# Index scores of a sparse-attention layer: the sum over heads moved from VectorE into PSUM, by products with diagonal matrices

## The chip, the cores and the metric

The kernel runs on one core of a Trainium2 chip. A core has five engines, each with its own in-order queue: TensorE (PE, matrix products; its weight loads are listed apart as PEld), VectorE (DVE), ScalarE (ACT), GpSimd (POOL) and SyncE (SP, which here only issues DMAs). The metric is the device time of one execution in microseconds, lower is better. TensorE is granted one of two clocks, 1.2 or 2.4 GHz; the profile gives the mean granted clock of a stretch as a share of the full one.

## The reference, cut to what matters

A decoder trunk of two layers works on 1024 tokens of width 1024, with 16 meta tokens ahead of them (1040 rows), in float32. The first layer picks, for every query, its 256 best keys by an index score, and then attends to those keys only. The changed part is the score:

```python
logits = jnp.einsum('qhd,sd->qhs', qi_blk, ki_s)              # 8 index heads of 64
score = jnp.einsum('qh,qhs->qs', w_blk, jax.nn.relu(logits))  # signed weight per query and head
score = jnp.where(causal, score, -jnp.inf)
_, idx = lax.top_k(score, topk)
```

A query block has 128 queries. Block b (0 to 7) sees L[b] = 16 + 128(b+1) keys. Block 0 needs no selection, so scores are computed for blocks 1 to 7, over 272, 400, 528, 656, 784, 912 and 1040 keys (4592 together).

## The kernel before

The program is written as Python generators (one per piece of work) that a helper, `weave`, pulls in turn in proportion to their number of steps. A scheduler then fixes the order in each engine's queue; tile pools with a given number of buffers decide what must wait for what.

The score stage, L538 to L549, weaves three things:

- `index(c)`: for the key and query columns of chunk c (three chunks of some 346 rows), five projections (L188, groups of 24 products: one "ki" and four "qi"). Each is copied out of PSUM (`raw_...`), rotated (`rope`, L344: four DMAs that swap halves into a `rot` tile, two POOL multiplications L350 and L351, an addition L352), and split into a high and a low float32r part, `kih`/`kil` and `qis` (ACT copies at L130, DVE subtractions L403 and L404).
- `scores(b)`, L441: for each head and each piece of at most 400 keys, two products L447 and L448 into a bank of tag "pt" (three buffers), a ReLU on ACT (L450) that multiplies by the absolute weight `wab`, into a tile `tm` (three buffers), and one DVE instruction that multiplies by the sign `wsg` and adds to the scores in SBUF (L452 for head 0, L454 for the others). At the end of a block DVE adds the causal mask to the last 128 columns (L458).
- with the last three blocks, the two projections of the attention keys (`k_evac`), whose norm needs a float32 product with the constant `sel` (L263) into a "pt" bank, then two ACT and four DVE instructions (L268 to L281; the bank is free after L276), and the first four rounds of `threshold(1, 5)`.

`threshold` finds the 256th best score of each row bit by bit: 31 rounds of counts (L470 on DVE for most blocks, L487 on ACT for blocks 3, 4 and 6), each round using the result of the last (L492, L493, L489). After the score stage, L550 weaves the other rounds of blocks 1 to 4, 16 rounds of blocks 5 to 7 and the eight query projections. Masks and attention follow.

PSUM has eight banks, four of tag "ps" (projections), three "pt", one "po". A plain float32 product appears in the trace as two records of L263 or L1300 each; a float32r product as one.

Of the kernel before, what the change touches and what calls it, by code (L numbers as in the profile page):

```python
# [10 lines left out]
F32 = mybir.dt.float32  # L11
# [3 lines left out]
OP = mybir.AluOpType  # L15
PSUM = bass.MemoryType.PSUM

P = 128
# [10 lines left out]
IH = 8  # L29
# [20 lines left out]
L = [NMETA + P * (b + 1) for b in range(NB)]  # L50
# [23 lines left out]
def chunks_of(n):  # L74
    parts = -(-n // 400)
    size = -(-n // parts)
    size += size % 2
    out, s = [], 0
    while s < n:
        out.append((s, min(size, n - s)))  # L80
        s += size
    return out
# [3 lines left out]
def trunk(ctx: ExitStack, tc: tile.TileContext, x, meta_tokens, attn_norm, mlp_norm, mlp_w1, mlp_w2,  # L86
          a_w_in, a_q_gain, a_k_gain, a_w_out, kv_norm, kv_w, kv_f_bias, kv_k_gain,
          b_w_q, b_q_gain, b_w_out, rope_cos, rope_sin, out):
    nc = tc.nc
    x = x[0]  # L90
    out = out[0]
# [13 lines left out]
    def bank(tag="ps"):  # L105
        n_ps[0] += 1
        return psum["p"].tile([P, 512], F32, tag=tag, name=f"ps{n_ps[0]}", bufs={"ps": 4, "pt": 3, "po": 1}[tag])
# [21 lines left out]
    def copy(dst, src, scale=1.0):  # L129
        nc.scalar.activation(dst, src, AF.Copy, scale=scale)  # L130
# [120 lines left out]
    HWID = SQW  # L251
# [42 lines left out]
    def scs(b):  # L294
        return sc[:, SC_OFF[b]:SC_OFF[b] + L[b]]
# [6 lines left out]
                            base=0, channel_multiplier=1)  # L302
# [37 lines left out]
    with tc.tile_pool(name="inw", bufs=2, reuse_waits="tile") as iw:  # L340
# [3 lines left out]
        def rope(src, dst, rows, name, s, m):  # L344
            rot = iw.tile([P, HWID], F32, tag="rot", name=f"rot{name}_{s}", bufs=3)[0:rows, 0:m]
            src, c, sn = src[0:rows, 0:m], rc[0:rows, s:s + m], rs[0:rows, s:s + m]
            for q in range(0, rows, 32):
# [6 lines left out]
        trifar = iw.tile([P, P], F32, name="trifar", bufs=1)  # L354
        nc.vector.memset(trifar, 0.0)
        nc.gpsimd.affine_select(out=trifar, in_=trifar, pattern=[[-1, P]], compare_op=OP.is_ge, fill=FAR,
                                base=0, channel_multiplier=1)
# [3 lines left out]
        wsg = iw.tile([P, NB, IH], F32, name="wsg", bufs=1)  # L361
        wab = iw.tile([P, NB, IH], F32, name="wab", bufs=1)

        def raw_tile(name, s):
            return iw.tile([P, HWID], F32, tag="raw", name=f"raw_{name}_{s}", bufs=5)

        def ends(s):
            return s == CH_A[-1][0]
# [1 line left out]
        def ki_evac(o, s, m):  # L370
            raw = raw_tile("ki", s)
            cs = slice(s, s + m)
            copy(raw[0:HD, 0:m], o[0:HD, 0:m])
            copy(wi[:, cs], o[HD:HD + IH, 0:m])
            rope(raw, raw[0:HD, 0:m], HD, "ki", s, m)
            split(kih[0:HD, cs], kil[0:HD, cs], raw[0:HD, 0:m])
            nc.sync.dma_start(f32(kih[HD:P, cs]), f32(kih[0:HD, cs]))
            nc.sync.dma_start(f32(kil[HD:P, cs]), f32(kil[0:HD, cs]))
            bs = [b for b in range(1, NB) if s < L[b] <= s + m]
            b0, b1 = bs[0], bs[-1] + 1  # L380

            def post():
                wt = bank("pt")
                for b in bs:
                    t0 = NMETA + P * b
                    nc.tensor.transpose(wt[:, b * IH:b * IH + IH], wi[:, t0:t0 + P], ident[0:IH, 0:IH])
                wv = wt[:, b0 * IH:b1 * IH].rearrange("p (b h) -> p b h", h=IH)
                sg, ab = wsg[:, b0:b1], wab[:, b0:b1]
                nc.vector.tensor_scalar(sg, wv, 0.0, 2.0, OP.is_ge, OP.mult)
                nc.vector.tensor_scalar(sg, sg, -1.0, None, OP.add)  # L390
                nc.vector.scalar_tensor_tensor(ab, wv, IH ** -0.5 * HD ** -0.5, sg, OP.mult, OP.mult)
            return post

        def qi_evac(mi):
            def evac(o, s, m):
                raw = raw_tile(f"qi{mi}", s)
                copy(raw[:, 0:m], o[:, 0:m])
                rope(raw, raw[:, 0:m], P, f"qi{mi}", s, m)
                e, o = s3[:, 2 * mi, s:s + m], s3[:, 2 * mi + 1, s:s + m]
                r0, r1 = raw[0:HD, 0:m], raw[HD:P, 0:m]  # L400
                copy(e[0:HD], r0)
                copy(o[HD:P], r1)
                nc.vector.tensor_tensor(e[HD:P], r0, f32(e[0:HD]), OP.subtract)  # L403
                nc.vector.tensor_tensor(o[0:HD], r1, f32(o[HD:P]), OP.subtract)  # L404
            return evac

        def k_evac(mi):
            def evac(o, s, m):
                raw = raw_tile(f"k{mi}", s)
                rest = head_norm(iw, o, s, m, G_AK, raw[:, 0:m], sqa[:, s:], 1)  # L410

                def post():
                    rest()
                    rope(raw, ka[:, mi, s:s + m], P, f"k{mi}", s, m)
                return post
            return evac
# [22 lines left out]
            return evac  # L439

        def scores(b):  # L441
            sb = scs(b)
            t0 = NMETA + P * b
            for h in range(IH):
                for s, m in chunks_of(L[b]):
                    o = bank("pt")
                    nc.tensor.matmul(o[:, 0:m], s3[:, h, t0:t0 + P], kih[:, s:s + m], start=True, stop=False)  # L447
                    nc.tensor.matmul(o[:, 0:m], s3[:, h, t0:t0 + P], kil[:, s:s + m], start=False, stop=True)  # L448
                    tm = iw.tile([P, 400], F32, tag="tm", name=f"tm{b}_{h}_{s}", bufs=3)
                    nc.scalar.activation(tm[:, 0:m], o[:, 0:m], AF.Relu, scale=wab[:, b, h:h + 1])  # L450
                    if h == 0:
                        nc.vector.tensor_scalar(sb[:, s:s + m], tm[:, 0:m], wsg[:, b, h:h + 1], None, OP.mult)  # L452
                    else:
                        nc.vector.scalar_tensor_tensor(sb[:, s:s + m], tm[:, 0:m], wsg[:, b, h:h + 1],  # L454
                                                       sb[:, s:s + m], OP.mult, OP.add)
                if h % 2:
                    yield
            nc.vector.tensor_tensor(sb[:, L[b] - P:], sb[:, L[b] - P:], trifar, OP.add)  # L458

        cand = att_in.tile([P, 2, NB], I32, name="cand")  # L460
        flip = att_in.tile([P, NB], I32, name="flip", bufs=1)
# [75 lines left out]
        nc.sync.dma_start(rs, rope_sin)  # L537
        weave((islice(pre, 3), 3), (index(0), 5))  # L538
        weave((pre, 2), (index(1), 5), (scores(1), 4))
        weave((index(2), 5), (chain(*[scores(b) for b in range(2, 5)]), 12))  # L540
        for i, g in enumerate((a_q_gain[0], a_k_gain[0], kv_k_gain, b_q_gain[0])):
            for half in range(2):
                nc.sync.dma_start(gains[HD * half:HD * half + HD, i:i + 1], g.rearrange("(p o) -> p o", o=1))
        rqb.append(bank("po"))
        va = att_in.tile([P, NW, AG, P], F32R, tag="va", name="va")
        thr1, thr2 = threshold(1, 5), threshold(5, NB)
        weave((chain(*[scores(b) for b in range(5, NB)]), 12),
              (chain(*[a_gemm(QW + mi * P, P, k_evac(mi), fine=True) for mi in range(2)]), 18),
              (islice(thr1, T1), T1))  # L549
# [547 lines left out]
    with tc.tile_pool(name="bw", bufs=2, reuse_waits="tile") as bw:  # L1097
# [95 lines left out]
        def qkv(t):  # L1193
            return chain(q_gemm(t), k_gemm(t), v_gemm(t))
# [123 lines left out]
        for u, (h, half, pr) in enumerate(units):  # L1318
# [5 lines left out]
            if half == 0 and h % 2 == 0:  # L1324
                if u:
                    run(fill)
                fill = qkv(t + 1) if t + 1 < NK else iter(())
# [67 lines left out]
```

## Time and profile before

| what | value |
|---|---|
| median of three timed runs | 2973.07 us (2971.38 to 2973.3) |
| profiled execution, its own time | 2966.22 us |
| its span, first to last instruction | 2964.4 us |
| busy in the span: PE / DVE / ACT / POOL | 2721.3 / 2109.0 / 1483.8 / 1309.8 us |
| mean granted TensorE clock | 0.96 |

The profiled execution is a single one; 1.8 us of its time lie outside its span, and it is 6.85 us under the median. Shares of busy time are means over very different stages: the score stage is the first 7% of the span. The recorded duration of a product includes its way through the array, so that the next one begins before it ends; how much of TensorE a product takes is seen in the distance from its start to the next start.

### The profile page before, as it was taken

To read this page: it belongs to the slowest core of one execution; us is meant where nothing else is said; L and a number is where in the kernel's file an instruction comes from. 1 tells how busy PE (TensorE), PEld (TensorE's weight loads), DVE (VectorE), ACT (ScalarE), POOL (GpSimd) and SP (SyncE) were. 2 spreads that over 40 slices of the span, in tenths; PEclk is the share of its full clock that TensorE was granted. 3 is DMA by queue.
4 is the path that set the end of the run, shared out by engine and by line. 5 is a ranking of instruction groups with operands and counts; after the bars stand their busy time and mean duration, and the time that the engine had idled before them with its cause. 6 is when DMAs were issued, how large, how long until landed. Compare 5 with 4: busy or idle time off the path is not lost.

```text
span 2964.4 us, 46393 instructions
## 1 busy us (share of the span) xinstructions
PE 2721.3 (92%) x16666; PEld 2390.6 (81%) x16666; DVE 2109.0 (71%) x4186; ACT 1483.8 (50%) x2828; POOL 1309.8 (44%) x1199
## 2 busy tenths in 40 slices
PE   6889788999889999999988999999897999989999
PEld 6779656778879998999978888888775788867777
DVE  7899989984664547666776778878857555567774
ACT  5767577885333334333434666666643333333332
POOL 2346344531455565222434555555515565542321
PEclk9999779999979999999999999999998999999999
DMA  5312200003224445444511111111322344454442
GB/s 171 78 46 70 52 19 1 1 1 101 79 90 155 147 141 194 137 123 129 157 61 49 51 51 51 51 51 51 101 64 68 124 157 146 149 181 151 148 135 71
DMA packets 243158, 281.96 MB, mean 95 GB/s; under 512 B 22272, under 2 KB 183872, under 8 KB 242928
## 3 DMA queue, kind: packets, MB, share of 16 engines
q1 hardware_dynamic: 242928, 279.01, 30.5%
q8 instruction: 131, 2.15, 0.3%
q14 instruction: 99, 0.81, 0.1%
HBM read 192.42 MB, written 67.63 MB: 88 GB/s over the span
## 4 chain that ended last, share of the span: by engine, by line
PE 55%; DVE 19%; DMA 8%; ACT 6%; issue 5%; POOL 5%; SPq 0%; POOLq 0%; ACTq 0%; DVEq 0%
PE ac L958 32%; PE ps L175 6%; DMA ld<-rdr 5%; PE ps L188 5%; DVE sc L470 3%; PE ps L697 2%; PE ps L662 2%; PE ps L1281 2%; PE ps L1303 2%; PE ps L717 1%; PE ps L720 1%; ACT bp L1259 1%; PE ps L1248 1%; DVE g L137 1%; DVE opc L137 1%
## 5 line engine op out<-in xcount | busy, mean ns | idle before, releaser
L958 PE MATMUL ac<-opc,g 128*128 128x260 f32 (+1 forms) x3456 | 580.6, 324 | 35.7 <-ACT q L130 12.0
L958 PEld LDWEIGHTS ac<-opc,g 128*128 128x128 f32 x3456 | 505.4, 192 | 94.9 <-ACT q L130 14.2
L958 PE MATMUL ac<-opb,g 128*128 128x260 f32 (+1 forms) x2304 | 390.1, 325 | 48.5 <-ACT opb L130 31.1
L958 PEld LDWEIGHTS ac<-opb,g 128*128 128x128 f32 x2304 | 336.3, 191 | 93.4 <-ACT opb L130 36.7
L958 PE MATMUL ac<-opa,g 128*128 128x260 f32 (+1 forms) x2304 | 396.1, 325 | 6.4 <-DVE osqa L238 4.4
L958 PEld LDWEIGHTS ac<-opa,g 128*128 128x128 f32 x2304 | 342.1, 193 | 42.5 <-DVE osqa L238 4.8
L950 POOL TENSOR_TENSOR t<-rb,t 128x512 f32<-128x512 f32 x128 | 190.9, 1491 | 342.8 <-DMA rb<-in_mlp_w_dram 270.6
L137 DVE TENSOR_TENSOR g<-t,g 128x512 fp32r<-128x512 f32 x256 | 224.3, 876 | 134.1 <-ACT g L130 131.4
L130 ACT ACTIVATE g<-t 128x512 fp32r<-128x512 f32 x256 | 161.0, 629 | 262.4 <-PE ac L958 156.9
L188 PE MATMUL ps<-xhb,wh 128*128 128x256 f32 (+5 forms) x640 | 208.6, 326 | 3.3 <-DVE z L1110 2.1
L188 PE MATMUL ps<-xhb,wl 128*128 128x256 f32 (+5 forms) x640 | 197.7, 309 | 0.0
L188 PE MATMUL ps<-xlb,wh 128*128 128x256 f32 (+5 forms) x640 | 196.8, 308 | 0.0
L950 POOL TENSOR_TENSOR t<-ra 128x512 f32<-128x512 f32 x64 | 98.3, 1535 | 179.5 <-DVE g L137 174.2
L137 DVE TENSOR_TENSOR g<-rb,g 128x512 fp32r<-128x512 f32 x128 | 111.7, 872 | 57.1 <-ACT g L130 57.0
L662 PE MATMUL ps<-ks,qs 128*128 128x264 f32 (+7 forms) x544 | 127.3, 347 | 24.7 <-DVE qs L588 12.7
L1239 POOL TENSOR_SCALAR bp<-bcb,cq 128x528 f32<-128x528 f32 (+7 forms) x128 | 103.6, 812 | 98.7 <-PE ps L1281 49.5
L130 ACT ACTIVATE bth<-ps 128x512 fp32r<-128x512 f32 (+4 forms) x224 | 110.5, 496 | 66.5 <-PE ps L1281 62.1
L1303 PE MATMUL ps<-bth,bvs 128*128 128x512 f32 (+2 forms) x420 | 134.3, 397 | 6.2 <-DVE qb L1310 5.0
L130 ACT ACTIVATE q<-ac 128x520 f32<-128x520 f32 (+1 forms) x96 | 57.6, 600 | 163.8 <-PE ac L958 158.8
L188 PEld LDWEIGHTS ps<-xhb,wh 128*128 128x128 f32 x640 | 122.5, 191 | 18.6 <-issue 9.8
L1263 POOL TENSOR_SCALAR bp<-bp,bnm 128x400 f32<-128x400 f32 (+7 forms) x128 | 101.1, 801 | 80.0 <-DVE bnm L1261 80.0
L130 ACT ACTIVATE wh<-wr 128x1024 fp32r<-128x1024 f32 (+1 forms) x84 | 87.4, 1040 | 93.8 <-PE ps L175 61.0
(353 smaller groups left out, 6775.4 us busy)
## 6 DMA issues: line engine op xcount, KB each, us to landing
ra<-in_mlp_w_dram SPq DMA_DIRECT2D x64, 512.0 KB, 3.9
rb<-in_mlp_w_dram SPq DMA_DIRECT2D x64, 512.0 KB, 4.3
ld<-rdr SPq DMA_DIRECT2D x56, 520.0 KB, 4.2
ld<-rdr SPq DMA_DIRECT2D x56, 512.0 KB, 4.0
rdr<-q SPq DMA_DIRECT2D x64, 260.0 KB, 2.0
rdr<-q SPq DMA_DIRECT2D x64, 256.0 KB, 2.3
rdr<-qs SPq DMA_DIRECT2D x48, 260.0 KB, 2.0
wr<-in_a_w_in_dram SPq DMA_DIRECT2D x24, 512.0 KB, 4.1
```

What stands on the lines that cost most here:

```text
L130: nc.scalar.activation(dst, src, AF.Copy, scale=scale)
L137: (nc.gpsimd if pool else nc.vector).tensor_tensor(lo, src, f32(hi), OP.subtract)
L175: nc.tensor.matmul(o[0:n, 0:m], a[:, k, 0:n], b[:, k, s:s + m], start=(k == 0 and j == 0), stop=(k == NK - 1 and j == 2))
L188: nc.tensor.matmul(o[0:n, 0:m], a[:, k, 0:n], b[:, k, s:s + m], start=(k == 0 and j == 0), stop=(k == NK - 1 and j == 2))
L470: nc.vector.tensor_scalar(eqb[:, 0:L[b]], scs(b), th, None, op, OP.add, accum_out=dst[:, b:b + 1])
L662: nc.tensor.matmul(o[:, 0:m], qs[:, h, :], kc, start=(v == 0), stop=(v == 1))
L697: nc.tensor.transpose(pt[0:rows, j * n:j * n + n], pr[j][q0:P, c0:c0 + rows], ident[q0:P, q0:P])
L950: nc.gpsimd.tensor_tensor(t, a, c, OP.subtract)
L958: nc.tensor.matmul(t[:, i, 0:m], a[:, j, :], c[:, j, o:o + m], start=start and j == 0 and v == 0, stop=stop and j == 3 and v == 2, skip_gr ...
L1239: nc.gpsimd.tensor_scalar(pj, cb[:, 0:n], 1.0, cq[:, b, h:h + 1], OP.mult, OP.add)
L1263: nc.gpsimd.tensor_scalar(pr[i], pr[i], nm[:, 3, i:i + 1], 0.0, OP.mult, OP.add)
L1303: nc.tensor.matmul(po[:, j0 * P:], v_kb, th[0:rows, v, j0 * P:], start=(kb == 0 and v == 0), stop=(kb == last and v == 1))
```

## The change

For each block a tile `dg` of eight 128x128 matrices is made on POOL, each with one head's 128 signs on its diagonal and zeros elsewhere (one `affine_select` over 1024 elements per row, from `wsg`; one buffer). Each ReLU tile is then multiplied on TensorE, as the moving operand, by its head's diagonal matrix (a plain float32 product, since `tm` and `dg` are float32), and the eight products accumulate in a bank `acc` of tag "ps". The product of a head is issued two heads after its ReLU. The loop order becomes pieces of keys outside, heads inside. When a piece is finished, ACT copies it to the scores, and DVE adds the mask straight from PSUM for the last 128 columns of a block. The `raw` tiles go from five buffers to four, since `dg` takes their place. The number of generator steps per block changes from 4 to 4, 4, 4, 4, 4, 6, 6 (blocks 1 to 7), with the step count that `weave` is told unchanged at 12 for the last three blocks.

```diff
-            return iw.tile([P, HWID], F32, tag="raw", name=f"raw_{name}_{s}", bufs=5)
+            return iw.tile([P, HWID], F32, tag="raw", name=f"raw_{name}_{s}", bufs=4)
...
-            for h in range(IH):
-                for s, m in chunks_of(L[b]):
+            dg = iw.tile([P, IH, P], F32, tag="dg", name=f"dg{b}", bufs=1)
+            sg = wsg[:, b].rearrange("p (h o) -> p h o", o=1).to_broadcast([P, IH, P])
+            nc.gpsimd.affine_select(out=dg, in_=sg, pattern=[[0, IH], [-1, P]], compare_op=OP.is_equal, fill=0.0,
+                                    base=0, channel_multiplier=1)
+            cs = chunks_of(L[b])
+            parts = 4 // len(cs) if len(cs) < 3 else 2
+            for s, m in cs:
+                acc = bank("ps")
+                tms = {}
+
+                def add(h):
+                    nc.tensor.matmul(acc[:, 0:m], dg[:, h], tms.pop(h)[:, 0:m], start=h == 0, stop=h == IH - 1)
+                for h in range(IH):
                     o = bank("pt")
...
-                    tm = iw.tile([P, 400], F32, tag="tm", name=f"tm{b}_{h}_{s}", bufs=3)
+                    tms[h] = tm = iw.tile([P, 400], F32, tag="tm", name=f"tm{b}_{h}_{s}", bufs=3)
                     nc.scalar.activation(tm[:, 0:m], o[:, 0:m], AF.Relu, scale=wab[:, b, h:h + 1])
-                    if h == 0:
-                        nc.vector.tensor_scalar(sb[:, s:s + m], tm[:, 0:m], wsg[:, b, h:h + 1], None, OP.mult)
-                    else:
-                        nc.vector.scalar_tensor_tensor(sb[:, s:s + m], tm[:, 0:m], wsg[:, b, h:h + 1],
-                                                       sb[:, s:s + m], OP.mult, OP.add)
-                if h % 2:
-                    yield
-            nc.vector.tensor_tensor(sb[:, L[b] - P:], sb[:, L[b] - P:], trifar, OP.add)
+                    if h > 1:
+                        add(h - 2)
+                    if (h + 1) % (IH // parts) == 0 and h < IH - 1:
+                        yield
+                add(IH - 2)
+                add(IH - 1)
+                e = m - P if s + m == L[b] else m
+                if e > 0:
+                    copy(sb[:, s:s + e], acc[:, 0:e])
+                if e < m:
+                    nc.vector.tensor_tensor(sb[:, s + e:s + m], acc[:, e:m], trifar, OP.add)
+                yield
```

On TensorE, in block 3 (pieces of 264 keys, during the projections of the last chunk), the queue before held score products with projection products (L188) spread among them:

```order
L447 MATMUL ps_1108<-kih,qis 128x264
L448 MATMUL ps_1108<-kil,qis 128x264
L447 MATMUL ps_1114<-kih,qis 128x264
L448 MATMUL ps_1114<-kil,qis 128x264
L188 MATMUL ps_1144<-xh,wh_1139 128x346
L447 MATMUL ps_1120<-kih,qis 128x264
L448 MATMUL ps_1120<-kil,qis 128x264
L188 MATMUL ps_1144<-xl,wh_1139 128x346
```

In the changed kernel the second piece of the same block begins so (L459 and L460 are the two score products, L456 is the product with the diagonal):

```order
L459 MATMUL ps_1103<-kih,qis 128x264
L460 MATMUL ps_1103<-kil,qis 128x264
L459 MATMUL ps_1108<-kih,qis 128x264
L460 MATMUL ps_1108<-kil,qis 128x264
L459 MATMUL ps_1113<-kih,qis 128x264
L460 MATMUL ps_1113<-kil,qis 128x264
L456 MATMUL ps_1102<-tm_0_264_1106,dg_1005 128x264
L459 MATMUL ps_1119<-kih,qis 128x264
L460 MATMUL ps_1119<-kil,qis 128x264
L456 MATMUL ps_1102<-tm_1_264_1111,dg_1005 128x264
```

A third product per head has come in, and the 24 products of a projection now stand together ahead of the piece.

On VectorE, at the end of the score stage (the last additions of block 7, then the first counts of blocks 6 and 7), the queue before was:

```order
L454 SCALAR_TENSOR_TENSOR sc<-tm_7_348_1997,wsg,sc 128x348
L454 SCALAR_TENSOR_TENSOR sc<-tm_7_696_2003,wsg,sc 128x344
L493 SCALAR_TENSOR_TENSOR cand<-dlt,flip 128x4
L470 TENSOR_SCALAR sc,cnt<-sc 128x912
L275 TENSOR_TENSOR ln_2016<-y_2017 128x346
L458 TENSOR_TENSOR sc<-sc,trifar 128x128
L276 SCALAR_TENSOR_TENSOR ln_2016<-ps_2014,ln_2016 128x346
L470 TENSOR_SCALAR sc,cnt<-sc 128x1040
```

and in the changed kernel (L473 is the mask addition from PSUM, L486 the count, L494 to L496 the start of the search for blocks 5 to 7):

```order
L281 SCALAR_TENSOR_TENSOR raw_k_694_1954<-ps_1852,gains,y_1959 128x346
L473 TENSOR_TENSOR sc<-ps_2024,trifar 128x128
L486 TENSOR_SCALAR sc,cnt<-sc 128x1040
L494 TENSOR_SCALAR dlt<-cnt 128x3
L486 TENSOR_SCALAR sc,cnt<-sc,cand 128x272
L495 TENSOR_SCALAR cand<-dlt 128x3
L496 TENSOR_SCALAR one<-dlt 128x3
L486 TENSOR_SCALAR sc,cnt<-sc,cand 128x400
```

The additions over heads are gone; the next round of blocks 1 to 4 (the count over 272 keys) still stands behind the last mask addition of block 7.

On POOL, the diagonal tile of block 2 (dg_856) stands in the changed kernel between the rope of the second and the third query projection of the middle chunk:

```order
L351 TENSOR_TENSOR raw_qi_348_701<-raw_qi_348_701,rc 128x346
L137 TENSOR_TENSOR wl_871<-wr_869,wh_870 128x8x72
L447 AFFINE_SELECT dg_856<-wsg 128x1024
L350 TENSOR_TENSOR rotqi_348_760<-rotqi_348_760,rs 128x346
L351 TENSOR_TENSOR raw_qi_348_758<-raw_qi_348_758,rc 128x346
```

It can only be written when the last product of block 1 has read the single buffer; before the change nothing stood there.

## Rows read from the trace of the kernel before

**Rows 1.** Busy time by stretch: start and end in us, its length, busy us (instructions) of PE, PEld, DVE, ACT and POOL, then the granted TensorE clock, DMA share and GB/s. The score stage ends near 195.

```profile
80.00:100.00 20.00, 16.54 (x92) 14.69 (x90) 18.71 (x32) 13.40 (x26) 6.24 (x6) 0.91 0.52 106
100.00:120.00 20.00, 15.55 (x87) 14.61 (x88) 17.15 (x33) 13.13 (x27) 6.04 (x6) 0.87 0.39 100
120.00:140.00 20.00, 18.60 (x98) 16.11 (x97) 18.37 (x36) 15.63 (x32) 5.71 (x5) 0.96 0.14 36
140.00:160.00 20.00, 16.98 (x100) 15.01 (x98) 19.86 (x45) 15.85 (x36) 7.48 (x7) 1.00 0.07 19
160.00:180.00 20.00, 16.93 (x91) 15.66 (x92) 18.85 (x41) 15.54 (x35) 5.28 (x6) 0.91 0.18 45
180.00:195.00 15.00, 12.63 (x73) 11.21 (x73) 15.00 (x25) 9.39 (x20) 7.33 (x6) 1.00 0.19 48
...
220.00:345.00 125.00, 114.18 (x734) 112.86 (x735) 117.45 (x307) 77.71 (x170) 69.82 (x73) 0.90 0.22 58
345.00:370.00 25.00, 9.36 (x47) 7.23 (x44) 24.02 (x66) 20.21 (x45) 3.87 (x6) 0.61 0.29 70
```

**Rows 2.** The chain of work that ended last, within 145 to 195 us: its shares by line, and one of its pieces (start, length, what).

```profile
by line: DVE sc L454 42.3%; DVE sc L470 13.1%; DVE ln L275 11.2%; DVE sc L452 6.4%; PE ps L188 5.2%; DVE ln L276 4.3%; DVE raw_k L281 2.9%; PE ps L447 2.9%; DVE y L280 2.6%; DVE sc L458 2.6%; PE ps L448 2.4%; DVE flip L489 2.1%; DVE dlt L49
...
185.01 7.63 DVE sc L454 x8
```

**Rows 3.** VectorE by line, 79.8 to 195 us: busy us and mean ns of one, idle before it.

```profile
L454 DVE SCALAR_TENSOR_TENSOR sc<-tm,wsg,sc 128x304 f32<-128x304 f32 (+7 forms) x92 | 58.5, 674 | 3.6 <-ACT tm L450 2.8
...
L452 DVE TENSOR_SCALAR sc<-tm,wsg 128x304 f32<-128x304 f32 (+6 forms) x13 | 6.3, 494 | 0.7 <-ACT tm L450 0.6
```

**Rows 4.** VectorE in order of time (start, us): the last mask addition of the scores, and the count after it.

```profile
194.09 0.28 DVE L458 TENSOR_TENSOR sc<-sc,trifar 128x128 f32<-128x128 f32 x1
...
194.72 1.22 DVE L470 TENSOR_SCALAR_CACHE_REDUCE sc<-sc 128x1040 f32<-128x1040 f32 x1
```

**Rows 5.** TensorE in order of time: the first product of block 2, and the last score product.

```profile
79.86 0.34 PE L447 MATMUL ps<-kih,qis 128*128 128x400 f32 x1
...
188.60 0.32 PE L448 MATMUL ps<-kil,qis 128*128 128x344 f32 x1
```

**Rows 6.** TensorE by line, 79.8 to 189.2 us.

```profile
L447 PE MATMUL ps<-kih,qis 128*128 128x304 f32 (+6 forms) x104 | 39.1, 379 | 17.8 <-ACT tm L450 7.8 <-DVE ln L276 6.9 <-DVE qis L403 2.9
L448 PE MATMUL ps<-kil,qis 128*128 128x304 f32 (+6 forms) x104 | 34.4, 334 | 0.0
L188 PE MATMUL ps<-xh,wl 128*128 128x346 f32 (+2 forms) x93 | 31.1, 334 | 0.0
L188 PE MATMUL ps<-xl,wh 128*128 128x346 f32 (+2 forms) x93 | 30.8, 331 | 0.0
L188 PE MATMUL ps<-xh,wh 128*128 128x346 f32 (+2 forms) x92 | 30.6, 333 | 0.0
L263 PE MATMUL ps<-sc,sel 128*128 128x346 f32 (+1 forms) x11 | 4.4, 478 | 0.0
```

**Rows 7.** TensorE in order of time at the full clock: one float32 product (L263, two records), then float32r products, each with its own start.

```profile
135.79 0.85 PE L263 MATMUL ps<-sc,sel 128*128 128x348 f32 x2
136.21 0.61 PE L447 MATMUL ps<-kih,qis 128*128 128x392 f32 x1
136.66 0.34 PE L448 MATMUL ps<-kil,qis 128*128 128x392 f32 x1
136.84 0.34 PE L447 MATMUL ps<-kih,qis 128*128 128x392 f32 x1
137.02 0.34 PE L448 MATMUL ps<-kil,qis 128*128 128x392 f32 x1
137.20 0.32 PE L188 MATMUL ps<-xh,wh 128*128 128x346 f32 x1
137.36 0.31 PE L188 MATMUL ps<-xl,wh 128*128 128x346 f32 x1
```

**Rows 8.** TensorE in order of time after a long wait (in brackets: idle before, and what ended it).

```profile
116.25 0.64 PE L447 MATMUL ps<-kih,qis 128*128 128x328 f32 x1 [4.14 <-ACT tm L450]
...
118.34 0.49 PE L188 MATMUL ps<-xh,wh 128*128 128x346 f32 x1
118.63 0.47 PE L447 MATMUL ps<-kih,qis 128*128 128x328 f32 x1
```

**Rows 9.** TensorE in order of time, much later in the kernel: one float32 product over 512 columns and what follows it.

```profile
2157.72 1.02 PE L1300 MATMUL ps<-bth,bvs 128*128 128x512 f32 x2
2158.58 0.60 PE L1281 MATMUL ps<-ident,bp 128*128 128x128 f32 x4
```

**Rows 10.** A rope: ScalarE copies a query projection out of PSUM, and later splits the rotated one (order of time); then the line L351 of the rope on POOL, over the score stage (ns min/median/max, first and last start).

```profile
103.60 0.44 ACT L130 ACTIVATE raw_qi<-ps 128x346 f32<-128x346 f32 x1
...
114.15 1.00 ACT L130 ACTIVATE qis<-raw_qi 64x346 fp32r<-64x346 f32 x2 [3.74 <-DVE raw_qi L352]
...
L351 POOL TENSOR_TENSOR raw_qi<-raw_qi,rc x11: 795/1056/1896, 46.9 to 129.8; 128x346 f32<-128x346 f32 x8, 128x348 f32<-128x348 f32 x3
```

**Rows 11.** The price of a mask made on POOL (before 20 us), and of the ReLUs on ScalarE (79.8 to 189.2 us).

```profile
L301 POOL TENSOR_SCALAR_AFFINE_SELECT tri<-tri 128x128 f32<-128x128 f32 x1 | 0.3, 292 | 0.6 <-DVE tri L300 0.6
...
L450 ACT ACTIVATE tm<-ps,wab 128x304 f32<-128x304 f32 (+6 forms) x103 | 52.1, 539 | 18.5 <-DVE sc L454 9.3 <-PE ps L448 7.2 <-DVE sc L452 1.4
...
L130 ACT ACTIVATE raw_qi<-ps 128x346 f32<-128x346 f32 x5 | 2.2, 449 | 0.8 <-PE ps L188 0.8
```

## The prediction

> **What bounds the kernel now.** I read the busy time by stretch first. From 80 to 195 us VectorE is busy 17 to 20 us of every 20, and TensorE too shows 15.5 to 18.6 [rows 1]. The chain of waits says which of the two ends last there: from 145 to 195 us most of it is VectorE, 42.3% the additions over heads (L454) alone, with eight in a row at the end [rows 2]. So the stage as it stands is VectorE's, and the change takes 92 + 13 instructions, 58.5 + 6.3 = 64.8 us, off it [rows 3]. That is the case for a gain.
>
> The busy share of TensorE hides the case against. A record of a product lasts some 330 ns, but the next one starts earlier. What a product takes is the distance between starts: 0.16 us for a projection product of 346 columns, 0.18 us for a score product of 392 columns [rows 7]. 392 columns at 2.4 GHz are 0.163 us, so a float32r product takes its columns at one per cycle and some 0.016 us.
>
> I take the stretch from the first product of block 2 (79.86) to the last score product (188.6 + 0.16 = 188.8), 108.9 us [rows 5]. TensorE's work in it, from the counts [rows 6]: 278 projection products x 0.159 = 44.2; 104 pairs of score products over 4592 - 272 = 4320 keys and 8 heads, that is 69,120 columns / 2.4 GHz = 28.8, and 208 x 0.016 = 3.3; 11 records of L263, so 5.5 products x 0.69 = 3.8. Together 80.1 us. TensorE therefore stands still, or runs at the half clock, for 28.8 us of the 108.9. The half clock explains at most 0.09 + 0.13 + 0.04 + 0.09 of 20 us, about 7 [rows 1]; it comes after long waits, as after the 4.14 us at 116.25, when 346 columns take 0.29 us [rows 8]. The rest are waits, of which the profile names 17.8 us before L447 [rows 6].
>
> VectorE finishes later than TensorE: the last mask addition ends at 194.09 + 0.28 = 194.37 [rows 4]. Behind it stands the bit search, which keeps VectorE busy 117.45 of the next 125 us and 24.02 of the last 25 while TensorE idles (9.36) [rows 1]. So whatever moves the moment of that last mask addition moves all that follows, one for one. My sum is about this moment.
>
> **The change part by part.** *The added products.* Each ReLU tile passes through TensorE again, as a plain float32 product. Such a product is two records, and two rows price it. Over 512 columns it holds TensorE from 2157.72 to 2158.58, 0.86 us [rows 9]: 1.68 ns a column, four cycles each at 2.4 GHz (0.853). Over 348 columns it starts at 135.79; the next product, of 392 columns, ends its stay at 136.66, so it began at 136.48, and the float32 product took 0.69 us [rows 7], 1.98 ns a column. At four cycles a column the 34,560 columns of blocks 2 to 7 cost 57.6 us; I add 0.05 us to each of the 104 products, between the two rows, and get 62.8. The bounds are 57.6 and 34,560 x 1.98 = 68.4. This is more than twice the 28.8 us in which TensorE does not work, so the products cannot hide: even with no wait left the stretch would be 80.1 + 62.8 us long.
>
> 13 projection products at the end of the stretch belong to the next stage, and in the new order stand behind all scores; they leave the stretch, 13 x 0.159 = 2.1 us. The work is then 80.1 - 2.1 + 62.8 = 140.8.
>
> *Block 1.* Its eight products of 272 columns (8 x 0.50 = 4.0 us) stand before 79.86, where TensorE has gaps. I take 1.5 us as the delay of the first product of block 2, from 0 to 4.0.
>
> *The removed additions.* They free VectorE; what this is worth is the part of the 28.8 us that goes. Where VectorE held TensorE up (a ReLU that waited for a `tm` tile: ACT idled 9.3 us on L454 [rows 11]; banks that waited for L276), the waits shrink. What is late next are the waits that are not VectorE's. I leave 17 us of them, estimated from the new order:
>
> - 6 us in block 2. The diagonal tile is a POOL mask of 1024 elements a row; 128 take 0.292 us [rows 11], so up to 2.3. There is one buffer, so it waits for the last product of block 1. Behind it on POOL stands the rope of a query projection, and behind that, on ACT, the copy-out of the next projection; its rope delays the last heads of block 2.
> - 3 us in blocks 3 and 4. ACT splits a rotated projection ahead of the next copies. From the copy-out to that split 10.5 us pass now (103.60 to 114.15, the last 3.74 in waiting for L352 [rows 10]); I take 8 without the additions ahead of L352. One projection and one piece of 264 keys (a head: 0.25 for the two score products, 0.49 for the new one) are 24 x 0.159 + 8 x 0.74 = 9.7 us of TensorE, so little of it shows.
> - 3 us at block 5, where four rounds of the search stand between its ReLUs on ACT.
> - 5 us at five norms: the third "pt" bank after L263 is free only after two ACT and two VectorE instructions.
>
> The bounds are 0 and all 28.8.
>
> *What costs nothing.* ACT gets 14 copies out of PSUM, 0.45 us or less each [rows 11]. It is busy at most 15.85 of 20 us [rows 1], and a ReLU (0.54 us) is shorter than a head's 0.74 us or more on TensorE, so the next head's products cover them; uncovered they would be 14 x 0.45 = 6.3 us. A `raw` tile lives some 12 us (copy-out 103.60 to split 115.15 [rows 10]), and one is taken every 8 us or more, so four buffers do as five did; were one missing, a copy-out would wait some 4 us. The mask addition (0.28) stays.
>
> *The sum.* 79.86 + 1.5 + 140.8 + 17 = 239.2, and 0.3 for the mask addition: 239.5, against 194.4 before. That is +45 us. The profiled execution's 2966.22 (span 2964.4 and 1.8 around it) becomes 3011; it lies 6.85 under the median of the runs, so I say **3018 us**.
>
> One rule would lighten this. The Trainium skill (GPSIMD Engine Reference, section 1, Specifications) says that GpSimd shares its SBUF interfaces with VectorE and contends with VectorE instructions that have two SBUF inputs, and L454 is of that kind. The trace has the spread that this would make: L351 takes 795 to 1896 ns, 1056 in the median [rows 10]. By the rule the two multiplications of a rope would each lose up to 0.26 us; with some four ropes on the path the sum would be 43 instead of 45.
>
> **The rivals.** *Most waits go.* With no wait and four cycles a column the end is at 79.86 + 80.1 - 2.1 + 57.6 + 0.3 = 215.8, +21 us: 2994. This is the least that the forecast's mechanism allows. I count it with the forecast.
>
> *All waits stay.* The old 28.8 us are there again, since ropes and norms stand in the new order with fewer projection products spread between the score products to cover them; with the upper price, 79.86 + 4 + 78.0 + 68.4 + 28.8 + 0.3 = 259.4, +65 us: 3038. For it speaks the new order on TensorE, in which scores and projections alternate in long runs; against it that VectorE is free and the clock falls only after long waits. Chance of more than +57: 0.12.
>
> *Faster, since a column costs one cycle.* If the diagonal products streamed like the score products, they would cost 34,560 / 2400 + 104 x 0.016 = 16.1 us. They would nearly fill what VectorE leaves: 79.86 + 78.0 + 16.1 + 10 + 0.3 = 184.3 with 10 us of waits, which is -10 us: 2963. It decides below 1 + 10 / 14.4 = 1.7 cycles a column. Both priced float32 rows say four, so 0.06.
>
> *The search fills the freed VectorE.* The 29 later rounds of blocks 1 to 4 need nothing from block 7. If they ran early, in the 64.8 us that VectorE gets free [rows 3], the next stage would give back the 45 us: 2973, no change. In the new order they stand behind the last mask addition in VectorE's queue, which is in order. 0.05.
>
> **How the numbers follow.** Less than 0.2% (6 us) of this kernel can't be told from no change. Forecast (+21 to +57) 0.77, all waits stay 0.12, one cycle 0.06, hidden 0.05. Faster 0.06, same 0.05, slower 0.89. The range goes from the lower bound, 2973.07 + 20, to the upper, 2973.07 + 65: 2993 to 3038.
>
> **What would show it.** Right: L456 appears in 224 records and its products lie about 0.45 to 0.7 us apart at the full clock; L473 of block 7 ends near 240 us; VectorE is about half busy from 100 to 235 and TensorE heads the chain there, with a granted clock near 1; the stretch from that L473 to the end of the kernel has its old length. Wrong: products with `dg` at one cycle a column; the counts of the search (L486) between the scores of block 7; gaps on TensorE of 25 us or more, or under 5; a stage after the scores whose length changes.

## The result, and the profile after

The changed kernel takes 3010.07 us in the median (3007.35 to 3011.36), the kernel before, timed beside it, 2973.19 (2971.38 to 2979.31): a ratio of 1.0127, 95% interval 1.0107 to 1.0148. It is slower by some 37 us; the forecast was slower by 45. The profiled execution took 3007.35 us, with a span of 3005.6.

The moment on which the sum was made, in order of time on VectorE and, below it, on TensorE (start, us, what; in brackets the idle time before and what ended it). It answers to [rows 4, 5]:

```profile
234.74 0.29 DVE L473 TENSOR_TENSOR sc<-ps,trifar 128x128 f32<-128x128 f32 x1 [12.08 <-ACT sc L130]
235.06 1.24 DVE L486 TENSOR_SCALAR_CACHE_REDUCE sc<-sc 128x1040 f32<-128x1040 f32 x1
```

```profile
80.50 0.39 PE L459 MATMUL ps<-kih,qis 128*128 128x272 f32 x1 [2.69 <-DVE xl L137]
...
85.50 0.34 PE L459 MATMUL ps<-kih,qis 128*128 128x400 f32 x1
...
230.95 0.58 PE L459 MATMUL ps<-kih,qis 128*128 128x344 f32 x1
231.37 0.32 PE L460 MATMUL ps<-kil,qis 128*128 128x344 f32 x1
231.53 0.74 PE L456 MATMUL ps<-tm,dg 128*128 128x344 f32 x2
231.84 0.58 PE L459 MATMUL ps<-kih,qis 128*128 128x344 f32 x1
...
232.42 1.90 PE L456 MATMUL ps<-tm,dg 128*128 128x344 f32 x6
233.89 0.58 PE L188 MATMUL ps<-xh,wh 128*128 128x348 f32 x1
234.31 0.32 PE L188 MATMUL ps<-xl,wh 128*128 128x348 f32 x1
```

The last mask addition ends at 234.74 + 0.29 = 235.03, against 194.37: +40.7 us. The span grew by 41.2. So all of the loss lies ahead of this moment. VectorE, which did the last eight additions without a pause before [rows 2], has now stood idle for 12.08 us, until ScalarE's copy of the sum came.

Busy time by stretch (columns as in [rows 1]):

```profile
80.00:100.00 20.00, 17.46 (x84) 13.64 (x85) 9.37 (x17) 11.93 (x23) 6.22 (x7) 1.00 0.45 99
100.00:120.00 20.00, 17.95 (x107) 16.12 (x106) 5.71 (x11) 10.42 (x22) 2.64 (x3) 1.00 0.21 52
...
140.00:160.00 20.00, 18.45 (x88) 14.90 (x88) 9.70 (x35) 14.99 (x34) 4.97 (x4) 1.00 0.13 35
...
180.00:200.00 20.00, 20.00 (x108) 17.19 (x107) 4.37 (x8) 10.86 (x23) 7.58 (x7) 1.00 0.16 40
...
220.00:235.00 15.00, 14.93 (x66) 11.39 (x67) 2.40 (x5) 8.84 (x18) 2.56 (x4) 1.00 0.18 47
260.00:385.00 125.00, 116.75 (x782) 114.86 (x780) 116.59 (x304) 78.01 (x169) 73.82 (x76) 0.95 0.22 59
385.00:410.00 25.00, 5.54 (x23) 4.62 (x24) 23.88 (x68) 19.45 (x39) 2.42 (x4) 0.52 0.26 65
```

TensorE fills the score stage, VectorE is busy less than half of each stretch (9.70 of 20 us is its most), toward the end a sixth, and the granted clock is 1.00 throughout. The two last rows are the stretches of 125 and 25 us of [rows 1], 40 us later: VectorE's busy times there are within 1 us of the old ones. The chain of waits from 150 to 235 us now runs over TensorE, and TensorE waits little (us in total, times, longest; 85.45 to 235 us):

```profile
by line: PE ps L456 43.9%; PE ps L188 19.6%; PE ps L459 11.2%; PE ps L460 9.8%; PE ps L263 4.0%; ACT sc L503 2.9%; ACT tm L462 2.6%; issue 2.1%; ACT sc L130 1.0%; ACT sc L258 0.9%; ACT ln L268 0.9%; ACT qis L130 0.6%; DVE sc L473 0.4%; DVE 
```

```profile
PE ps L456 <- ACT tm L462: 5.7, 6, 1.6
PE ps L263 <- ACT sc L258: 1.4, 1, 1.4
PE ps L459 <- DVE qis L403: 1.3, 1, 1.3
PE ps L459 <- ACT tm L462: 0.4, 1, 0.4
```

### The profile page after: what moved, and what is told of

It reads as the page before. It is cut to its first block, busy times and chain, and to the rows that moved or that the text cites. A ratio compares the mean times of both kernels' runs of the same rounds, so it can differ in the third digit from the quotient of the medians.

```text
span 3005.6 us, 46714 instructions
## 1 busy us (share of the span) xinstructions
PE 2774.4 (92%) x16890; PEld 2427.3 (81%) x16890; DVE 2045.7 (68%) x4074; ACT 1491.3 (50%) x2842; POOL 1313.8 (44%) x1206
## 4 chain that ended last, share of the span: by engine, by line
PE 58%; DVE 16%; ACT 7%; DMA 6%; POOL 4%; issue 4%; ACTq 0%; POOLq 0%; DVEq 0%; SPq 0%
PE ac L974 32%; PE ps L175 6%; PE ps L188 6%; DMA ld<-rdr 5%; DVE sc L486 2%; PE ps L678 2%; PE ps L713 2%; PE ps L1297 2%; PE ps L733 2%; PE ps L1319 2%; PE ps L456 1%; PE ps L736 1%; DVE g L137 1%; POOL bp L1255 1%; DVE opa L137 1%
## 5 line engine op out<-in xcount | busy, mean ns | idle before, releaser
L974 PE MATMUL ac<-opc,g 128*128 128x260 f32 (+1 forms) x3456 | 580.8, 324 | 32.1 <-ACT q L130 11.1
L974 PEld LDWEIGHTS ac<-opc,g 128*128 128x128 f32 x3456 | 506.0, 192 | 91.4 <-ACT q L130 13.2
L974 PEld LDWEIGHTS ac<-opb,g 128*128 128x128 f32 x2304 | 337.0, 191 | 93.4 <-ACT opb L130 36.8
L188 PE MATMUL ps<-xhb,wh 128*128 128x256 f32 (+5 forms) x640 | 208.7, 326 | 6.5 <-DVE qb L281 3.2
L188 PE MATMUL ps<-xhb,wl 128*128 128x256 f32 (+5 forms) x640 | 197.9, 309 | 0.0
L188 PE MATMUL ps<-xlb,wh 128*128 128x256 f32 (+5 forms) x640 | 197.0, 308 | 0.0
L678 PE MATMUL ps<-ks,qs 128*128 128x264 f32 (+7 forms) x544 | 127.8, 344 | 26.8 <-DMA ks<-ks 18.2
L188 PEld LDWEIGHTS ps<-xhb,wh 128*128 128x128 f32 x640 | 122.5, 191 | 22.1 <-issue 9.7
L130 ACT ACTIVATE q<-ac 128x520 f32<-128x520 f32 (+1 forms) x96 | 57.6, 600 | 164.6 <-PE ac L974 162.2
```

Source lines behind the costliest of these rows:

```text
L188: nc.tensor.matmul(o[0:n, 0:m], a[:, k, 0:n], b[:, k, s:s + m], start=(k == 0 and j == 0), stop=(k == NK - 1 and j == 2))
L678: nc.tensor.matmul(o[:, 0:m], qs[:, h, :], kc, start=(v == 0), stop=(v == 1))
L974: nc.tensor.matmul(t[:, i, 0:m], a[:, j, :], c[:, j, o:o + m], start=start and j == 0 and v == 0, stop=stop and j == 3 and v == 2, skip_gr ...
```

## The experiments

All runs have the loop order of the changed kernel; "after" in the tables and below is that kernel itself. I give for each the stretch on TensorE from block 2's first product to the last product of the scores, and the work in it: counted projection products x 0.159, 32.1 us of score products, norm products (346 columns) x 0.577, and the added products at four cycles a column (57.6 us for eight heads; in the one-pass version 16.1). What remains is called waits. By this count before has 79.5 us of work and 29.4 of waits (the prediction had 80.1 and 28.8, with a norm product at 0.69). The counts of projection products take in two or three at the edges of the stretch in every row, which is 0.3 to 0.5 us of work too much and as much of waits too little. The tail is from the last product to the end of the last mask addition. The last two columns are differences from before: of the end of that addition, and of the medians of executions timed beside each other (us).

| kernel | heads on VectorE | first product | work | waits | tail | end of mask | later than before | median later by |
|---|---|---|---|---|---|---|---|---|
| before | 8 | 79.86 | 79.5 | 29.4 | 5.6 | 194.37 | - | - |
| e_order | 8 | 80.80 | 83.8 | 28.8 | 4.8 | 198.27 | +3.9 | +4.2 |
| e_hyb2 | 6 | 80.34 | 92.6 | 28.2 | 3.6 | 204.70 | +10.3 | +13.2 |
| e_hyb4 | 4 | 85.02 | 106.8 | 18.4 | 2.6 | 212.90 | +18.5 | +20.3 |
| e_half | 0 | 84.03 | 107.0 | 19.4 | 0.9 | 211.33 | +17.0 | +15.0 |
| e_onepass | 0 | 81.13 | 94.9 | 17.4 | 0.9 | 194.33 | 0.0 | +9.3 |
| after | 0 | 85.50 | 135.6 | 13.0 | 0.9 | 235.03 | +40.7 | +36.9 |
| e_w16 | 0 | 84.11 | 134.1 | 11.5 | 0.9 | 230.57 | +36.2 | +36.8 |
| e_t1_20 | 0 | 86.36 | 135.6 | 16.7 | 0.9 | 239.63 | +45.3 | +51.9 |

The waits are a remainder, so a row always adds up; what the runs test is whether the remainder stays put when the work is changed. The profile of each kernel is one execution. The lengths behind the mask addition lie between 2765.8 and 2785.3 us, and 2770.0 in before, so that the later part can move an execution by up to 15 us (in e_onepass). The first product varies too: after, e_w16 and e_t1_20 have the same queues up to it and start it at 85.50, 84.11 and 86.36.

### The order alone: e_order

The additions go back to VectorE; the order of the loops, the two heads of lag and the four `raw` buffers stay.

```diff
-                nc.tensor.matmul(acc[:, 0:m], dg[:, h], tms.pop(h)[:, 0:m], start=h == 0, stop=h == IH - 1)
+                if h == 0:
+                    nc.vector.tensor_scalar(sb[:, s:s + m], tms.pop(h)[:, 0:m], wsg[:, b, h:h + 1], None, OP.mult)
+                else:
+                    nc.vector.scalar_tensor_tensor(sb[:, s:s + m], tms.pop(h)[:, 0:m], wsg[:, b, h:h + 1],
+                                                   sb[:, s:s + m], OP.mult, OP.add)
```

> The changed kernel without the products: the new loop order, the four raw tiles and the lag of two heads stay, but the ReLU tiles are multiplied and added on VectorE as before (no dg, no acc, no copy from PSUM). Theory A (the float32 products fill TensorE, and this is the whole loss): the loss goes, 2965 to 2982 us, and the last mask addition of block 7 ends at 187 to 203 us. Rival B (the loss comes from the new order and its waits: scores and projections in long runs, ropes behind ReLUs on ACT): 2995 us or more.

2976.87 us, ratio 1.0015 (1.0002 to 1.0029), theory A. The last mask addition:

```profile
197.36 0.91 DVE L470 TENSOR_TENSOR sc<-sc,trifar 128x128 f32<-128x128 f32 x1
```

It ends 3.9 us later than before. The order, the lag and the missing `raw` buffer together cost about a tenth of the loss (4.2 us of 36.9 by the medians, 0.6 to 8.6 by the interval). The rest comes with the products, their diagonal tiles and the copies of the sums; the run with one-pass products parts these.

### Half the products: e_half

```diff
+                t = tms.pop(h)
-                nc.tensor.matmul(acc[:, 0:m], dg[:, h], tms.pop(h)[:, 0:m], start=h == 0, stop=h == IH - 1)
+                if h % 2:
+                    nc.tensor.matmul(acc[:, 0:m], dg[:, h], t[:, 0:m], start=h == 1, stop=h == IH - 1)
```

> Only the odd heads are summed (the even heads' ReLU tiles are made and not used, so that part of the score is left out). 56 products instead of 112. Theory A: half of 61.2 us at four cycles a column, 30.6, leaves TensorE's queue, and most of it the time: 2978 to 2988 us. Rival B (waits, not products): under 10 us less than the changed kernel, 3000 us or more.

2987.7 us, ratio 1.0055 (1.0029 to 1.0081), just inside theory A. The last mask addition:

```profile
211.04 0.29 DVE L475 TENSOR_TENSOR sc<-ps,trifar 128x128 f32<-128x128 f32 x1 [8.16 <-ACT sc L130]
```

28.8 us of products less end the stage 23.7 us earlier: 28.8 and 1.5 of an earlier start, less 6.4 by which the waits grew and 0.2 for one projection product more. So the stage is TensorE's list, and growing waits take back a fifth of what is saved.

### Products in one pass: e_onepass

```diff
-            dg = iw.tile([P, IH, P], F32, tag="dg", name=f"dg{b}", bufs=1)
+            dg = iw.tile([P, IH, P], F32R, tag="dg", name=f"dg{b}", bufs=1)
-                    tms[h] = tm = iw.tile([P, 400], F32, tag="tm", name=f"tm{b}_{h}_{s}", bufs=3)
+                    tms[h] = tm = iw.tile([P, 400], F32R, tag="tm", name=f"tm{b}_{h}_{s}", bufs=3)
```

> ReLU tiles and diagonal tiles are float32r instead of float32, so that a product is one record (the scores are rounded, which leaves part of their precision out). Theory A: a product costs its columns once, 36,736 x 0.417 ns = 15.3 us and 0.016 each instead of 61.2, some 44 us less of TensorE's work; ropes and norms then hold it up more often, so 30 to 44 us less time: 2966 to 2980 us. Rival B: 3000 us or more, since every wait, copy and diagonal tile is still there.

2981.97 us, ratio 1.0034 (1.0022 to 1.0047), 2 us above theory A's range. TensorE in order of time and, below it, the last mask addition on VectorE:

```profile
178.12 0.32 PE L459 MATMUL ps<-kih,qis 128*128 128x348 f32 x1
178.28 0.32 PE L460 MATMUL ps<-kil,qis 128*128 128x348 f32 x1
178.44 0.32 PE L456 MATMUL ps<-tm,dg 128*128 128x348 f32 x1
178.60 0.32 PE L459 MATMUL ps<-kih,qis 128*128 128x348 f32 x1
```

```profile
194.04 0.29 DVE L473 TENSOR_TENSOR sc<-ps,trifar 128x128 f32<-128x128 f32 x1 [6.34 <-ACT sc L130]
```

A product with the diagonal now holds TensorE 0.16 us, as a score product does, and is one record. The last mask addition ends at 194.33, where it ended before: 40.7 us come back when nothing but the passes of the products is changed. ReLUs (539 ns in the mean, 536 in after) and diagonal tiles (1.09 us) last as long as in after. So what the score stage loses are the four cycles a column. Even so there is no gain: with 16.1 us of products and no addition on VectorE the stage is as long as with all additions there. By the medians 27.6 of the 36.9 us come back. The other 9.3 are lost behind the stage, and where is only partly seen (below).

### The search in the freed VectorE: e_t1_20

```diff
-T1 = 4
+T1 = 20
```

> The changed kernel with 20 instead of 4 rounds of the search of blocks 1 to 4 woven into the score stage, where VectorE now idles. Theory A with VectorE still the bound of the stage after it: 16 rounds of some 1.8 us move into idle time, the score stage keeps its length, the next gets 20 to 30 us shorter: 2980 to 2992 us. Rival C (the rounds' sign counts on ACT, 2.0 us a round, hold up the ReLUs and so TensorE): the score stage grows by what the next one gives, 3005 to 3015 us.

3024.65 us, ratio 1.0182 (1.0155 to 1.0209): all expectations missed. Sixteen more rounds of the search ran between the scores, the stage ended 4.6 us later, and what stands behind it did not get shorter. TensorE's waits from 235 to 440 us, first of after, then of this kernel:

```profile
PE ps L678 <- DMA ks<-ks: 18.2, 1, 18.2
PE ps L436 <- ACT sc L426: 6.5, 4, 2.7
```

```profile
PE ps L436 <- ACT sc L426: 33.3, 9, 11.8
PE ps L678 <- DMA ks<-ks: 16.3, 1, 16.3
```

ScalarE's waits in the same stretch, in the same order:

```profile
ACT sc L503 <- DVE cand L509: 36.8, 23, 7.3
```

```profile
ACT sc L503 <- DVE cand L509: 61.0, 27, 12.2
```

The next stage interleaves the remaining rounds of blocks 1 to 4 (29 in after, 13 here), 16 steps of the search of blocks 5 to 7, and the query projections. With fewer short rounds the long ones stand closer together. ScalarE does a part of each round's counts (L503), in order, and waits for VectorE's next candidate; behind it in its queue stands the copy of a projection for the norm (L426), for which TensorE waits: 33.3 us instead of 6.5. The first attention product (L678), at 401.5 us in after, came at 439.0, and the last one at 716.5 and not 701.2: of the 37.5 us that it was late, 22 came back within attention. So the free time of VectorE was no gain in this order; the interleave of the next stage would have to be made anew, which was not tried.

### Additions on both engines: e_hyb4 and e_hyb2

The first NPE heads (4, then 2) go through TensorE; VectorE adds the others, beginning with the sum in PSUM.

```diff
-                nc.tensor.matmul(acc[:, 0:m], dg[:, h], tms.pop(h)[:, 0:m], start=h == 0, stop=h == IH - 1)
+                if h < NPE:
+                    nc.tensor.matmul(acc[:, 0:m], dg[:, h], tms.pop(h)[:, 0:m], start=h == 0, stop=h == NPE - 1)
+                else:
+                    nc.vector.scalar_tensor_tensor(sb[:, s:s + m], tms.pop(h)[:, 0:m], wsg[:, b, h:h + 1],
+                                                   acc[:, 0:m] if h == NPE else sb[:, s:s + m], OP.mult, OP.add)
...
-                if e > 0:
-                    copy(sb[:, s:s + e], acc[:, 0:e])
                 if e < m:
-                    nc.vector.tensor_tensor(sb[:, s + e:s + m], acc[:, e:m], trifar, OP.add)
+                    nc.vector.tensor_tensor(sb[:, s + e:s + m], sb[:, s + e:s + m], trifar, OP.add)
```

> Heads 0 to 3 are summed by products with the diagonals, heads 4 to 7 by VectorE, which starts from the sum in PSUM, so that no copy is left. Theory A (TensorE is the path of the stage as soon as its list is longer than the stage was, and its waits stay near the 20 us that the runs with half the products and with one-pass products leave): first product of block 2 at 84, work 80.1 - 2.1 + 28.8 = 106.8, waits 20, last mask addition at 210 to 216, time 2985 to 2995. Rival B (the two engines share the additions, and the shorter lists of both end sooner than the VectorE list did): last mask addition at 194 or before, time at most 2973. Rival C (the four VectorE additions at the end of a chunk become a wait of 1 to 2 us for each of ten chunks): last mask addition at 222 to 230, time 2998 to 3008.

> The same with two heads on TensorE and six on VectorE. The products then cost TensorE 14.4 us, as much as the one-pass products of all heads did, and VectorE loses a quarter of its additions (13 of some 52 us over 64 us saved per whole). Theory A (TensorE's own list with its waits is what holds the stage, and a shorter VectorE list doesn't shorten it): last mask addition at 194 to 201, time 2970 to 2984. Rival B (VectorE was the limit and gains): last mask addition at 182 to 190, time 2961 to 2970.

2989.85 us, ratio 1.0063 (1.004 to 1.0086), with four heads on TensorE: theory A in place and time. 2982.7 us, ratio 1.0043 (1.0028 to 1.0057), with two: no gain either, theory A in time, but the mask addition at 204.70, later than A's 194 to 201. The table says why: with six heads on VectorE TensorE still waits 28.2 us, nearly as in before, and the 14.4 us of products come on top, less the shorter tail. With four heads the waits are 18.4 us, so that of the 14.4 us of products that come in between the two runs the stage shows 8.2. Neither of the two splits finds a balance of the engines. Other splits, and splits with one-pass products, were not run.

VectorE's end in the version with two heads, in order of time:

```profile
199.82 0.57 DVE L460 SCALAR_TENSOR_TENSOR sc<-tm,wsg,ps 128x344 f32<-128x344 f32 x1 [1.17 <-ACT tm L467]
200.50 3.88 DVE L460 SCALAR_TENSOR_TENSOR sc<-tm,wsg,sc 128x344 f32<-128x344 f32 x5
204.41 0.29 DVE L476 TENSOR_TENSOR sc<-sc,trifar 128x128 f32<-128x128 f32 x1
```

It is idle for 1.17 us in the last chunk, waiting for a ReLU, where before it went through eight additions without a pause [rows 2].

### Another mixture: e_w16

```diff
-        weave((chain(*[scores(b) for b in range(5, NB)]), 12),
+        weave((chain(*[scores(b) for b in range(5, NB)]), 16),
```

> The changed kernel with the share of the scores in the interleave with the key projection told as 16 steps and not 12, so that the pieces of the scores come in another mixture with the projection's products. Theory A (TensorE's list, 148.6 us from block 2's first product of which 13 are waits, sets the end, whatever the mixture): last mask addition at 232 to 238, time 3003 to 3015. Rival (a good part of the 13 us of waits comes from products standing too close behind their ReLU): last mask addition at 225 to 231, time 2996 to 3003, or as much later where the mixture is worse.

3006.29 us, ratio 1.0118 (1.0098 to 1.0138), not to be told from after's 1.0127. The time is theory A's, but the mask addition, at 230.57, lies in the rival's range: 4.5 us earlier than in after. 1.5 us of that are projection and norm products that moved behind the scores, 1.5 fewer waits, and 1.4 an earlier start, which the edit can't have made, since the queues are the same up to there. The mixture decides some 3 us, not the forty.

## Why the prediction was right, step by step

It forecast 3018 us, from 2993 to 3038, and slower. The mechanism was its own: the products cannot hide, TensorE becomes the path, and all behind the last mask addition moves along. Its terms:

- *The first product of block 2* was put at +1.5 us (0 to 4.0). It came 5.6 us later, outside its bounds: this is the term that failed. The prediction let gaps of TensorE take in most of the eight products of block 1, and they took in next to nothing: from 45 us to this product the profile names 9.2 us of TensorE's waits in before and 8.5 in after, and eight products of 272 columns at four cycles a column are 3.6 us. One wait grew by 1.0 us. A score product of block 1, which waits for the split `xl`, stood at 80.50 after 2.69 us of waiting; before it stood here:

```profile
76.96 0.40 PE L447 MATMUL ps<-kih,qis 128*128 128x272 f32 x1 [1.69 <-DVE xl L137]
```

  In before VectorE made this split at 76.22, ahead of a rope's addition (L352); now it came behind that addition, which took 1.70 us beside a split on POOL and not 0.52 as at 74.30:

```profile
78.06 1.41 POOL L137 TENSOR_TENSOR wl<-wr,wh 128x576 fp32r<-128x576 f32 x1
78.14 1.70 DVE L352 TENSOR_TENSOR raw_qi<-raw_qi,rotqi 128x346 f32<-128x346 f32 x1 [1.71 <-POOL raw_qi L351]
79.77 1.27 DVE L137 TENSOR_TENSOR xl<-ps,xh 128x512 fp32r<-128x512 f32 x2
```

  The last us is not traced; it is no more than the start differs between kernels with the same queues (84.11 to 86.36).
- *The products* were put at 62.8 us (57.6 to 68.4). A head of block 7 with 344 columns repeats every 231.84 - 230.95 = 0.89 us; less two score products of 0.16 it is 0.57, which is 344 x 4 / 2.4 GHz = 0.573. The 0.05 us added to each of the 104 products is not there: 57.6, -5.2 us against the sum.
- *The work that left the stretch* was 2.1 us; 267 projection products are in it instead of 278, 1.7 us less.
- *The waits* were put at 17 us; 13.0 are left, -4. The profile names 8.8 of them. 5.7 are six products with the diagonal that wait for a ReLU. Four of these, 3.4 us, are in blocks 3 and 4, for which 3 us were counted, but at three of the four (106.70, 117.25 and 127.98) it isn't the split of a rotated projection that holds ScalarE up: it splits weights and copies a finished projection before it makes the first ReLUs of a piece. On ScalarE, and then on TensorE:

```profile
104.78 1.06 ACT L130 ACTIVATE wh<-wr 128x1024 fp32r<-128x1024 f32 x1 [3.74 <-PE ps L188]
105.75 0.43 ACT L130 ACTIVATE raw_qi<-ps 128x346 f32<-128x346 f32 x1
106.08 1.22 ACT L462 ACTIVATE tm<-ps,wab 128x264 f32<-128x264 f32 x3
```

```profile
106.70 0.68 PE L456 MATMUL ps<-tm,dg 128*128 128x264 f32 x2 [1.07 <-ACT tm L462]
```

  For block 2's rope I counted 6 us; the only wait for a rotated projection is 1.3 (L403). The diagonal tile of 1024 elements took 1.09 us and not up to 2.3 (shown below), and though it waited 7.2 us for the last product of the block ahead, no product in this stretch waited for it. The search's rounds (3) and the norms (5) show 1.4 at L263 and one product, at 150.81, that waits 1.55 us for a ReLU behind a count of the search and a split.
- *The sum.* +4.1 of start, -5.2 of products, -4 of waits, +0.4 of projection products, -0.3 of norm products (0.577 us each and not 0.69), and 0.6 us more between the last product and the end of the mask addition than the 0.3 counted: 235.0 instead of 239.5. The start that was set too low is covered by products and waits that were set too high, which is luck; no term is off by more than 5.2. The time is right within 8 us. The other 4 of these come from the step from the profiled execution to the median: 6.85 us were added, as in before, and 2.7 lie between the two in after.
- *What was to show it.* L456 has 224 records; TensorE heads the chain; the clock is 1.00; the stage behind is as long as before (3005.6 - 235.03 = 2770.6, before 2964.4 - 194.37 = 2770.0). Only VectorE, foreseen about half busy, is busy less: 3.5 to 9.7 of 20 us.
- *The rivals.* One cycle a column was worked out as 10 us faster. The one-pass version made exactly these products and gained nothing: the rival had put the waits at 10 us, and 17.4 were left. "All waits stay" holds in the runs with six and eight heads on VectorE (28.2 and 28.8 us), and not with four or none. The search in the freed VectorE fails by more than its place in the queue: sixteen of its rounds, moved there, gave nothing back.

POOL's mask lines in after, over the kernel (ns min/median/max), and the rope's multiplications over the stage:

```profile
L447 POOL TENSOR_SCALAR_AFFINE_SELECT dg<-wsg x7: 1081/1092/1096, 34.5 to 205.4; 128x1024 f32<-128x1024 f32 x7
```

```profile
L351 POOL TENSOR_TENSOR raw_qi<-raw_qi,rc 128x346 f32<-128x346 f32 x6 | 5.0, 840 | 0.0
L350 POOL TENSOR_TENSOR rotqi<-rotqi,rs 128x346 f32<-128x346 f32 x6 | 5.0, 839 | 26.3 <-DMA rotqi<-raw_qi 19.3 <-DVE wl L137 6.9
```

The same six L351 took 1047 ns each in before and take 840 now, the six L350 902 and 839: 0.27 us a rope, without the additions on VectorE. The rule of the Trainium skill that the prediction weighed (GPSIMD Engine Reference, section 1, Specifications) agrees with that in direction, at half the price that was taken for it.

What stays open is the part behind the scores in e_onepass: 9.3 us in the medians with the stage as long as before. In its trace the first attention product stands 175.1 us behind the mask addition, in before 165.1. VectorE's three short instructions of a search round (L505, L508, L509) take 346, 467 and 433 ns in the mean from 200 to 420 us, the same three (L489, L492, L493) 288, 377 and 410 in before, and 299, 328 and 360 in after; over 48 rounds that is 8 us more than in before, and 12 more than in after. That these are the lost us was not tested by a run.

## What to carry to other kernels

Count the work of the engine that would receive an operation, by the distance between starts, before its busy share: here TensorE had 29 us free in 109, and the products needed 58, since a plain float32 product cost four cycles a column. How much the giving engine is relieved of does not decide: VectorE lost 65 us of work, more than the products cost, and the stage grew all the same. What must be shorter than the old stage is the receiver's list with the new work and the waits that stay: with products at one cycle a column (16 us) it was just as long as before, and in neither of the two splits was it shorter. The free time won on VectorE gave nothing in the one order tried, in which ScalarE's queue then held TensorE up.

## What the runs showed of the hardware

- A float32 product of 344 columns takes 0.57 us with its neighbours close by, which is four cycles a column at 2.4 GHz (0.573) and no more; a float32r product of 348 columns takes 0.16.
- A POOL mask over 1024 elements takes 1.09 us, one over 128 0.292 [rows 11]: not in proportion, 0.89 ns an element beyond the first 128.
- A short VectorE instruction can last as long as a POOL instruction beside it. In e_t1_20, in order of time:

```profile
290.96 2.39 POOL L137 TENSOR_TENSOR wl<-wr,wh 128x1024 fp32r<-128x1024 f32 x1 [0.28 <-ACT wh L130]
291.01 2.36 DVE L508 TENSOR_TENSOR dlt<-cnt,lim 128x3 int32<-128x3 f32 x1
293.31 0.93 POOL L352 TENSOR_TENSOR qa<-raw_q,rotq 128x346 f32<-128x346 f32 x1
293.40 0.86 DVE L509 SCALAR_TENSOR_TENSOR cand<-dlt,flip 128x3 int32<-128x3 int32 x1
```

  L508 on three elements a partition takes 163 ns in the median and 2.36 us here: it ends with POOL's split, and L509 with POOL's next addition. Both read two SBUF operands. L505, which reads one, is lengthened too: 0.86 us at 249.57 in after, where 0.17 is usual. The Trainium skill (Trainium Architecture — The Big Picture, What this means for kernel authors) calls the port pair that the two engines share an exclusive lock, not a bandwidth split; these four lines agree.
- The granted clock was 1.00 from 80 to 235 us in after, with 13 us of waits, and 0.87 to 1.00 in before, with 29.
